# The first stage of a decoder block laid down in a fixed order for every engine

## The chip, the cores and the metric

The kernel runs on one core of a Trainium2 chip. The metric is device microseconds from start to end of one execution. Five engines work side by side, each through its own list of instructions in order: PE (TensorE, the matmuls), ACT (ScalarE), DVE (VectorE), POOL (GpSimd) and SP (SyncE, which here only issues loads and stores). An instruction that waits for another engine or for a transfer holds up all that stand behind it in its own list.

## What is computed

One decoder layer on 512 tokens of width 1024, in float32. The stage that is changed is the first: the norm of x, its transposes, and the projection to values and branch gates.

```python
h = rmsnorm(x, norm_mix[l])
proj = h @ w_in[l]
(qa, ka, va, qb, kc, vc, ksl, vsl, kw, vw, g_nsa, g_a, g_b) = jnp.split(proj, IN_OFFSETS, axis=-1)
y_a = swa_sink_attention(heads(qa, A_HEADS), heads(ka, A_KV_HEADS), heads(va, A_KV_HEADS),
                         attn_sinks[l], table_a)
...
nsa_gates = jax.nn.sigmoid(g_nsa).reshape(bsz, seq, B_KV_GROUPS, B_HEADS // B_KV_GROUPS, 3)
...
merged = jax.nn.sigmoid(g_a) * (y_a @ w_up_a[l]) + jax.nn.sigmoid(g_b) * (y_b @ w_up_b[l])
x = x + merged @ w_out[l]
h = rmsnorm(x, norm_ffn[l])
ug = causal_dwconv(h @ w_ffn_in[l], conv_w[l], conv_b[l])
...
x = x + (jax.nn.silu(g) * u) @ w_ffn_out[l]
```

The attentions add a bias from a table of 32 distance buckets by 16 heads (`rel_bias_table`).

## The kernel before

Each float32 operand of a matmul is split into a high part (a rounded copy, made on ACT, L79) and a low part (what is left, made on DVE or POOL, L80), and a product is three matmuls: high by high, high by low, low by high (L91 to L93).

The **first stage** takes the tokens in four blocks of 128. For each block `norm_x` (L152) squares both halves of x on ACT (`junk`), sums and scales them on DVE (`ssq`), takes the power -0.5 on POOL (`rstd_n`), multiplies x by it and by the norm's weights on DVE (L161), and has PE transpose the eight 128 by 128 pieces into two banks (`tp_x`, two groups of four), whose high and low parts (`xTh`, `xTl`) ACT and DVE take out. The norm's weights reach all partitions by a matmul of a column of ones with the loaded row (`gam`, L112, from `grow`). `values` (L171) then multiplies a block with the weights of the value and gate columns, 408 of them (`wvr` as loaded, in two halves of the model width; `wvh`, `wvl` split): 24 matmuls `v` for each block, 96 in all. The block's result is taken out by ACT and DVE in turn as `VA`, `VB` and the gates (`eg`); only then is its bank free.

Behind it come the **projections** of keys and queries (`p_ka`, `p_qa`, `p_kc`, ...), 24 matmuls for each 128 columns, with weights loaded through a ring of three (`raw_ka`, `raw_qa`, ...) and split (`hl_ka`, ...), and then, between the projections, the attention. `p_ka` takes the bank that the third token block's values have left.

The **distance table** is a matmul of the bucket table with a one-hot matrix (`pg`, L419, from `tab` and `og`, in pieces of 384, 512 and 128 columns) that ACT copies out (L420); SP writes it 32 times over to memory (`gdr`, L421, 1 MB from 8 partitions) and reads it back shifted (`TA`, L427).

All loads are issued by SP. In its queue each one waits until the load eight issues ahead of it has landed. What stands where in an engine's list is set by a scheduler that goes by priorities and a model of the times; in the first stage too. The low part of half of `wvr` and of `raw_ka` is split off on POOL (`POOLJ`, L26, L191).

Of the kernel before, what the change touches and what calls it, by code (L numbers as in the profile page):

```python
# [48 lines left out]

def hybrid(tc, x, wv, wblk, w1, w2, wua, wub, wout, wfi, wfo, nmix, nffn, nfin, sinks, par, table, onehot, out):  # L50
# [9 lines left out]
    with es:  # L60
# [16 lines left out]

        def split(hi, lo, src, eng=None):
# [24 lines left out]
        for h in range(2):  # L103
            sl = slice(h * 512, (h + 1) * 512)
            nc.sync.dma_start(xt[0][:, sl], x[0:P, sl])
            if h == 0:
                nc.sync.dma_start(grow, nmix)
        ones = C.tile([1, P], F32, name="ones")
        V.memset(ones, 1.0)
        gam = [bank("sc", f"gam{h}") for h in range(2)]  # L110
        for h in range(2):
            T.matmul(gam[h], ones, grow[:, h * 512 : (h + 1) * 512], start=True, stop=True)  # L112
# [3 lines left out]
        nc.sync.dma_start(wvr[0], wv[0])  # L116
        nc.sync.dma_start(xt[1], x[P : 2 * P])
        nc.sync.dma_start(wvr[1], wv[1])
        for t in range(2, NT):
            nc.sync.dma_start(xt[t], x[t * P : (t + 1) * P])  # L120
# [738 lines left out]
```

## Time and profile before

| | |
|---|---|
| three runs | 776.62, 777.75 and 781.49 us, median 777.75 |
| the profiled execution: span from first to last instruction | 779.1 us |
| instructions | 9688 |
| mean granted clock of TensorE over the span | 0.982 |

Of the profiled execution only the span is recorded, not a time of its own beside it. The span lies within the three runs, 1.4 us above their median, so the profile can stand for a usual run; a difference worked out against its span is carried over to the median.

### The profile page before, as it was taken

Reading aid. Unit: us, or ns where it says so; the run is one execution under the profiler, and the core shown is the slowest. Engines: PE = TensorE matmul, PEld = TensorE weight load, DVE = VectorE, ACT = ScalarE, POOL = GpSimd, SP = SyncE. Lnnn points to the kernel's source line nnn. Section 1 sums busy time; section 2 is a strip of 40 time slices with the busy share of each in tenths; the row PEclk is TensorE's granted clock in tenths of the full one; section 3 lists DMA queues with packets and bytes.
Section 4 is the critical chain, followed back from the end, with each engine's and each line's share of the span. In section 5 each row is a group of like instructions: output and inputs, shape, how many; then the busy total and the mean of one; then the engine's idle time right before and its main releaser. Section 6 shows DMA issues by size and latency. Waiting matters only on the chain.

```text
span 779.1 us, 9688 instructions
## 1 busy us (share of the span) xinstructions
PE 755.7 (97%) x3566; PEld 622.9 (80%) x3566; DVE 458.7 (59%) x921; ACT 370.9 (48%) x684; POOL 156.0 (20%) x125
## 2 busy tenths in 40 slices
PE   7999989899999999989999999999999999999996
PEld 5788778787887878768889888888888888888885
DVE  5527988746875567668755666565665555224123
ACT  7335685645666765546333534444443443213113
POOL 5024536324423344321500000000000000002001
PEclk9899998999999999999999999999999999999998
DMA  8463335421121211123502423323232233232302
GB/s 301 94 138 119 101 99 165 125 82 55 32 77 55 82 56 52 66 99 128 170 1 82 136 89 100 105 85 108 84 107 93 96 109 119 98 108 81 109 28 108
DMA packets 24182, 76.74 MB, mean 98 GB/s; under 512 B 3748, under 2 KB 4900, under 8 KB 24134
## 3 DMA queue, kind: packets, MB, share of 16 engines
q1 hardware_dynamic: 24134, 76.12, 30.6%
q8 instruction: 28, 0.46, 0.2%
q14 instruction: 20, 0.16, 0.1%
HBM read 72.96 MB, written 3.15 MB: 98 GB/s over the span
## 4 chain that ended last, share of the span: by engine, by line
PE 90%; DVE 6%; POOL 1%; issue 1%; ACT 1%; DMA 1%; SPq 0%; POOLq 0%; DVEq 0%; ACTq 0%
PE ug L92 10%; PE ug L93 10%; PE ug L91 10%; PE fo L753 5%; PE fo L752 5%; PE fo L754 5%; PE pT L454 3%; PE up L91 2%; PE p_gb L93 2%; PE up L93 2%; PE up L92 2%; PE p_gb L91 2%; PE p_gb L92 2%; PE wo L92 2%; PE wo L91 2%; PE wo L93 2%
## 5 line engine op out<-in xcount | busy, mean ns | idle before, releaser
L92 PE MATMUL ug<-hTl,hl_fi 128*128 128x512 f32 (+1 forms) x376 | 141.1, 375 | 0.0
L93 PE MATMUL ug<-hTh,hl_fi 128*128 128x512 f32 (+1 forms) x376 | 141.1, 375 | 0.0
L91 PE MATMUL ug<-hTh,hl_fi 128*128 128x512 f32 (+1 forms) x376 | 140.9, 376 | 0.0
L92 PEld LDWEIGHTS ug<-hTl,hl_fi 128*128 128x128 f32 x376 | 70.8, 188 | 12.9
L91 PEld LDWEIGHTS ug<-hTh,hl_fi 128*128 128x128 f32 x376 | 70.6, 188 | 12.9
L93 PEld LDWEIGHTS ug<-hTh,hl_fi 128*128 128x128 f32 x376 | 70.8, 188 | 12.6
L736 ACT ACTIVATE cv<-ug,prm 128x512 f32<-128x512 f32 x44 | 34.4, 782 | 96.0 <-PE ug L93 96.0
L737 DVE SCALAR_TENSOR_TENSOR cv<-ug,prm,cv 128x511 f32<-128x511 f32 x44 | 33.0, 750 | 77.0 <-ACT cv L736 76.9
L753 PE MATMUL fo<-hl_fo,AH 128*128 128x512 f32 x176 | 68.5, 389 | 0.0
L752 PE MATMUL fo<-hl_fo,AH 128*128 128x512 f32 x176 | 67.3, 389 | 0.0
L80 DVE TENSOR_TENSOR hl_fo<-raw_fo,hl_fo 128x1024 fp32r<-128x1024 f32 x22 | 27.1, 1235 | 64.6 <-ACT hl_fo L79 64.6
L778 POOL TENSOR_TENSOR X<-X,nfin 128x512 f32<-128x512 f32 x4 | 5.2, 1318 | 296.7 <-ACT junk L776 296.7
L80 DVE TENSOR_TENSOR ptl<-pT,pth 128x512 fp32r<-128x512 f32 (+4 forms) x62 | 41.8, 685 | 30.5 <-ACT pth L79 25.5
L80 DVE TENSOR_TENSOR hl_fi<-raw_fi,hl_fi 128x1024 fp32r<-128x1024 f32 x44 | 53.5, 1217 | 1.8 <-ACT hl_fi L79 1.8
L79 ACT CAST hl_fo<-raw_fo 128x1024 fp32r<-128x1024 f32 x22 | 23.2, 1054 | 65.6 <-PE fo L754 65.6
L376 ACT ACTIVATE Pb<-Pb,nmb 128x512 f32<-128x512 f32 (+3 forms) x64 | 35.9, 561 | 35.2 <-DVE nmb L447 34.9
L754 PE MATMUL fo<-hl_fo,AL 128*128 128x512 f32 x128 | 49.8, 389 | 0.0
L79 ACT CAST hl_fi<-raw_fi 128x1024 fp32r<-128x1024 f32 x44 | 45.7, 1041 | 2.4 <-PE wo L93 2.4
L79 ACT CAST pth<-pT 128x512 fp32r<-128x512 f32 (+4 forms) x62 | 35.2, 583 | 20.3 <-PE pT L454 15.6
L587 POOL TENSOR_TENSOR Pb<-Pb,smb 128x512 f32<-128x512 f32 (+3 forms) x32 | 25.9, 829 | 65.2 <-DVE smb L571 45.3
L752 PEld LDWEIGHTS fo<-hl_fo,AH 128*128 128x128 f32 x176 | 33.0, 188 | 6.9
L753 PEld LDWEIGHTS fo<-hl_fo,AH 128*128 128x128 f32 x176 | 33.0, 188 | 6.8
(308 smaller groups left out, 1727.3 us busy)
## 6 DMA issues: line engine op xcount, KB each, us to landing
raw_fi<-in_wfi_dram SPq DMA_DIRECT2D x44, 512.0 KB, 3.3
raw_fo<-in_wfo_dram SPq DMA_DIRECT2D x22, 512.0 KB, 3.2
raw_w<-in_w_dram SPq DMA_DIRECT2D x8, 512.0 KB, 3.6
raw_ga<-in_wblk_dram SPq DMA_DIRECT2D x8, 512.0 KB, 3.3
raw_gb<-in_wblk_dram SPq DMA_DIRECT2D x8, 512.0 KB, 3.2
raw_wo<-in_wout_dram SPq DMA_DIRECT2D x5, 512.0 KB, 3.7
raw_qa<-in_wblk_dram SPq DMA_DIRECT2D x4, 512.0 KB, 5.0
raw_qb<-in_wblk_dram SPq DMA_DIRECT2D x4, 512.0 KB, 6.1
```

The lines of the kernel that those rows point to most:

```text
L79: A.copy(hi, src)
L80: (eng or V).tensor_tensor(lo, src, f(hi), op=ALU.subtract)
L91: T.matmul(ps, wh, xh, start=start, stop=False)
L92: T.matmul(ps, wh, xl, start=False, stop=False)
L93: T.matmul(ps, wl, xh, start=False, stop=stop)
L376: last_exp[0] = A.activation(a[0], a[1], AF.Exp, **k)
L587: G.tensor_tensor(pr[r][:, :n], pr[r][:, :n], sm[:, r : r + 1].to_broadcast([P, n]), op=ALU.mult)
L736: A.activation(c, ps, AF.Identity, scale=cw(2, blk), bias=cb(blk))
L737: V.scalar_tensor_tensor(c[:, 1:], ps[:, : S - 1], cw(1, blk), c[:, 1:], op0=ALU.mult, op1=ALU.add)
L752: T.matmul(po[t], ah, wh, start=(k == 0), stop=False)
L753: T.matmul(po[t], ah, wl, start=False, stop=False)
L754: T.matmul(po[t], al, wh, start=False, stop=(k == NF - 1))
```

## The change

The first stage is written out instruction by instruction, under a switch that makes the scheduler keep that order on every engine. Against before:

- PE begins with twelve transposes of the identity (`early`) whose results nobody reads; then come `gam`, the whole table product `pg` (in banks of the tag `pt`, not `sc`), and then the first block of x.
- The row of the norm, the bucket table and the one-hot matrix are loaded from ACT's queue; the other loads stay on SP. The sinks (`nsink`) are loaded ahead of the first projection's weights, the table is written (`gdr`) right behind the small loads `cx`.
- The value weights are split in four pieces of 816 columns: high parts on ACT between the other steps, low parts on DVE; POOL splits nothing in this stage, and `ka` leaves `POOLJ`, so that its low part is made on DVE too.
- The high and low parts of projection weights may not stand ahead of the last block's transposed parts on their engines (`issue_after`).

```diff
         def split(hi, lo, src, eng=None):
-            A.copy(hi, src)
-            (eng or V).tensor_tensor(lo, src, f(hi), op=ALU.subtract)
+            xparts.append(A.copy(hi, src))
+            xparts.append((eng or V).tensor_tensor(lo, src, f(hi), op=ALU.subtract))
...
-        norm_x(0)
-        VA = slot(16, [P, NT, 2, P], F32R, "VA")
-        for h in range(2):
-            split(wvh[h], wvl[h], wvr[h], (G, None)[h])
-        for t in range(1, NT):
-            norm_x(t)
-            values(t - 1)
-        values(NT - 1)
...
+        def wv_hi(h, c):
+            A.copy(wvh[h][:, 2 * c : 2 * c + 2], wvr[h][:, 2 * c : 2 * c + 2])
+
+        def wv_lo(h, c):
+            cs = slice(2 * c, 2 * c + 2)
+            V.tensor_tensor(wvl[h][:, cs], wvr[h][:, cs], f(wvh[h])[:, cs], op=ALU.subtract)
...
+        with tc.manual_schedule():
...
+            nc.scalar.dma_start(grow[:, :D], nmix)
+            nc.scalar.dma_start(tab[:32], table)
+            nc.scalar.dma_start(oh, onehot)
...
+            for i in range(3):
+                pw = bank("pt", f"early{i}")
+                for c in range(4):
+                    T.transpose(pw[:, c * P : (c + 1) * P], ident, ident)
+            gam = [bank("sc", f"gam{h}") for h in range(2)]
...
+            pgs = []
+            for c0, c1, h0 in ((0, ZA, 0), (ZA, ZA + 512, 8), (ZA + 512, ZA + ZW, 8)):
+                pgs.append((bank("pt", f"pg{c0}"), c0, c1))
+                T.matmul(pgs[-1][0][:8, : c1 - c0], tab[:, h0 : h0 + 8], oh[:, c0:c1], start=True, stop=True)
+            squares(0)
+            scaled(0)
+            for pg, c0, c1 in pgs:
+                A.copy(gsb[:, c0:c1], pg[:8, : c1 - c0])
+            for c in range(2):
+                wv_hi(0, c)
+                transposed(xt[0], xTh, xTl, 0, c, "x")
+            values(0, 0, False)
+            squares(1)
+            wv_lo(0, 0)
+            wv_lo(0, 1)
+            values(0, 0, True)
+            wv_hi(1, 0)
+            wv_hi(1, 1)
+            scaled(1)
+            values(0, 1, False)
+            for t in range(1, NT):
+                transposed(xt[t], xTh, xTl, t, 0, "x")
+                if t == 1:
+                    wv_lo(1, 0)
+                    wv_lo(1, 1)
+                if t + 1 < NT:
+                    squares(t + 1)
+                values(t - 1, 1, True)
+                transposed(xt[t], xTh, xTl, t, 1, "x")
+                xlast = xparts[-2:]
+                if t + 1 < NT:
+                    scaled(t + 1)
+                values(t, 0, False)
+                values_out(t - 1)
+                values(t, 0, True)
+                values(t, 1, False)
+            values(NT - 1, 1, True)
+            values_out(NT - 1)
...
         def filler():
-            i, nxt = 0, jobs[0][1]()
+            with tc.issue_after(xlast[0].ins), tc.issue_after(xlast[1].ins):
+                i, nxt = 0, jobs[0][1]()
```

`squares`, `scaled` and `values_out` are the parts of `norm_x` and `values` under names of their own; `values(t, h, low)` is the part of block t's 24 matmuls that uses half h of the model width, without or with the weights' low part.

The beginning of PE's list, before (`_86` and the like are buffer numbers; `x_79` holds the first two blocks):

```order
L112 MATMUL gam_86<-grow,ones 128x512
L112 MATMUL gam_87<-grow,ones 128x512
L144 MATMUL tp_x_0_127<-ident,x_79 128x128 x4
L144 MATMUL tp_x_1_135<-ident,x_79 128x128 x4
L177 MATMUL v_173<-wvh_92,xTh_110 128x408 x4
L177 MATMUL v_173<-wvh_92,xTl_112 128x408 x4
L177 MATMUL v_173<-wvh_93,xTh_111 128x408 x4
L177 MATMUL v_173<-wvh_93,xTl_113 128x408 x4
```

Here the first block's transposes follow the norm's broadcast at once.

On PE after, a dozen transposes and the table product come first; `x_75` holds the first two blocks there:

```order
L212 MATMUL early_121<-ident 128x128 x4
L212 MATMUL early_126<-ident 128x128 x4
L212 MATMUL early_131<-ident 128x128 x4
L215 MATMUL gam_136<-grow 128x512
L215 MATMUL gam_137<-grow 128x512
L219 MATMUL pg_140<-og,tab 8x384
L219 MATMUL pg_142<-og,tab 8x512
L219 MATMUL pg_144<-og,tab 8x128
L131 MATMUL tp_x_0_162<-ident,x_75 128x128 x4
L131 MATMUL tp_x_1_170<-ident,x_75 128x128 x4
L174 MATMUL v_177<-wvh_83,xTh_91 128x408 x4
L174 MATMUL v_177<-wvh_83,xTl_93 128x408 x4
```

The table product, which stood between the second and third block's transposes, now stands ahead of the first, behind twelve transposes that are new.

The end of the stage in ACT's list, before (`v_292` is the third block's bank, `v_325` the fourth's):

```order
L79 CAST xTh_110<-tp_x_0_277 128x4x128
L79 CAST VB<-v_233 128x4x64
L79 CAST xTh_111<-tp_x_1_285 128x4x128
L182 ACTIVATE eg_262<-v_233 128x24
L79 CAST VA<-v_292 128x2x64
L79 CAST VB<-v_292 128x4x64
L182 ACTIVATE eg_321<-v_292 128x24
L79 CAST VA<-v_325 128x2x64
L79 CAST VB<-v_325 128x4x64
L182 ACTIVATE eg_354<-v_325 128x24
L319 CAST KA<-p_ka 64x512
```

Between the third block's `VA` and its gates stands only its `VB`.

The same place on ACT after (`v_306` is the third block's bank, `tp_x_1_346` the last transposes of x):

```order
L81 CAST xTh_91<-tp_x_0_335 128x4x128
L81 CAST xTh_92<-tp_x_1_346 128x4x128
L81 CAST VA<-v_306 128x2x64
L81 CAST hl_ka<-raw_ka 128x1024
L81 CAST hl_qa_404<-raw_qa_402 128x1024
L81 CAST hl_qa_455<-raw_qa_453 128x1024
L81 CAST VB<-v_306 128x4x64
L183 ACTIVATE eg_366<-v_306 128x24
L81 CAST VA<-v_353 128x2x64
L81 CAST VB<-v_353 128x4x64
L183 ACTIVATE eg_390<-v_353 128x24
L378 CAST KA<-p_ka 64x512
```

Three casts of projection weights, which stood earlier, between the first blocks, now stand between the third block's `VA` and its `VB` and gates; DVE's three low parts stand in the same place in its list.

SP's queue around the table's write, before:

```order
L412 DMA og<-in_onehot_dram 33x1024
L415 DMA cx<-in_w_dram 128x2x64 x4
L85 DMA raw_qa_432<-in_wblk_dram 128x1024
L85 DMA raw_kc<-in_wblk_dram 128x1024
L85 DMA raw_qa_509<-in_wblk_dram 128x1024
L421 DMA gdr<-og 8x32x1024
L85 DMA raw_w_0_0_610<-in_w_dram 128x1024
L427 DMA TA<-gdr 32x8x256 x4
```

Three weight loads stand ahead of the write, one between it and `TA`.

The same place in SP's queue after:

```order
L87 DMA raw_qa_402<-in_wblk_dram 128x1024
L466 DMA cx<-in_w_dram 128x2x64 x4
L468 DMA gdr<-og 8x32x1024
L87 DMA raw_qa_453<-in_wblk_dram 128x1024
L87 DMA raw_kc<-in_wblk_dram 128x1024
L474 DMA TA<-gdr 32x8x256 x4
L87 DMA raw_qa_530<-in_wblk_dram 128x1024
L87 DMA raw_w_0_0_631<-in_w_dram 128x1024
```

The write of the table has moved ahead of the weights of `qa1` (`raw_qa_432` before, `raw_qa_453` after) and of `kc`. Behind this, from `p_ka` on, the lists of PE, ACT, DVE and POOL are the same as before.

## Rows read from the trace of the kernel before

**Rows 1.** page, part 1: busy us (share of the span) and instructions per engine

```profile
PE 755.7 (97%) x3566; PEld 622.9 (80%) x3566; DVE 458.7 (59%) x921; ACT 370.9 (48%) x684; POOL 156.0 (20%) x125
```

**Rows 2.** windows, one stretch: busy us per engine, granted clock, DMA share, GB/s

```profile
40.28:100.00 59.72, 58.13 (x282) 47.74 (x282) 39.66 (x102) 33.54 (x75) 23.90 (x17) 0.97 0.44 118
```

**Rows 3.** chain of waits, 0 to 57 us: start us, us, what

```profile
9.08 3.69 POOL wvl L80
...
13.06 2.13 POOL rstd_n L137
...
30.61 0.44 PE tp_x L144 x4
...
32.23 8.21 PE v L177 x44
```

**Rows 4.** timeline of PE: start us, us, what, idle before and releaser

```profile
3.35 3.75 PE L112 MATMUL gam<-grow,ones 1*128 1x512 f32 x4 [3.35 <-DMA grow<-in_nmix_dram]
7.71 1.97 PE L144 MATMUL tp_x<-ident,x 128*128 128x128 f32 x8 [0.61 <-DVE x L161]
9.54 1.73 PE L177 MATMUL v<-wvh,xTh 128*128 128x408 f32 x4
...
14.83 1.65 PE L177 MATMUL v<-wvl,xTh 128*128 128x408 f32 x8
...
21.10 3.15 PE L419 MATMUL pg<-og,tab 33*8 33x384 f32 x4 [1.39 <-DVE x L161]
...
40.28 0.40 PE L91 MATMUL p_ka<-xTh,hl_ka 128*128 128x512 f32 x1
```

**Rows 5.** windows of 1 us, PE alone: busy us, granted clock, DMA share, GB/s

```profile
21.00:22.00 1.00, 0.90 (x2) 0.50 0.68 172
```

**Rows 6.** timeline of POOL

```profile
1.02 0.29 POOL masks.py:199 TENSOR_SCALAR_AFFINE_SELECT ident<-ident 128x128 f32<-128x128 f32 x1
```

**Rows 7.** timeline of ACT

```profile
7.45 1.55 ACT L79 CAST wvh<-wvr 128x1632 fp32r<-128x1632 f32 x1 [1.60 <-DMA wvr<-in_wv_dram]
...
10.01 0.58 ACT L79 CAST xTh<-tp_x 128x512 fp32r<-128x512 f32 x1
...
14.06 0.60 ACT L156 ACTIVATE junk<-x 128x512 f32<-128x512 f32 x1
...
16.68 1.05 ACT L79 CAST hl_ka<-raw_ka 128x1024 fp32r<-128x1024 f32 x1
...
28.20 0.26 ACT L420 COPY og<-pg 8x128 f32<-8x128 f32 x1 [2.28 <-PE pg L419]
...
37.48 0.19 ACT L182 ACTIVATE eg<-v 128x24 f32<-128x24 f32 x1 [0.49 <-DVE VB L80]
```

**Rows 8.** timeline of DVE

```profile
12.91 1.86 DVE L80 TENSOR_TENSOR wvl<-wvr,wvh 128x1632 fp32r<-128x1632 f32 x1
15.21 1.41 DVE L161 SCALAR_TENSOR_TENSOR x<-x,rstd_n,gam 128x512 f32<-128x512 f32 x2 [0.45 <-POOL rstd_n L137]
...
21.63 0.68 DVE L80 TENSOR_TENSOR xTl<-tp_x,xTh 128x512 fp32r<-128x512 f32 x1
...
23.16 1.21 DVE L80 TENSOR_TENSOR hl_qa<-raw_qa,hl_qa 128x1024 fp32r<-128x1024 f32 x1
...
37.03 0.42 DVE L80 TENSOR_TENSOR VB<-v,VB 128x256 fp32r<-128x256 f32 x1 [0.44 <-ACT VB L79]
```

**Rows 9.** tile view of tab, 0 to 75 us: time from issue to landing

```profile
DMA to landing us min/median/max: 8.0/8.0/8.0
```

**Rows 10.** timeline of SP, the queue of loads

```profile
16.33 0.35 SPq L85 DMA_DIRECT2D raw_qa<-in_wblk_dram  x1
...
28.48 0.31 SPq L421 DMA_DIRECT2D gdr<-og  x1
28.89 0.33 SPq L85 DMA_DIRECT2D raw_w<-in_w_dram  x1
```

**Rows 11.** tile view of raw_w, 28 to 52 us: time from issue to landing

```profile
DMA to landing us min/median/max: 22.7/22.7/22.7
```

More of the change, by code (lines that the diff above doesn't have):

```diff
@@ L102, in hybrid @@
         xt = [(x01, x23)[t // 2][:, t % 2] for t in range(NT)]
-        for h in range(2):
[L104 to L112, printed above, removed]
+        halves = [slice(0, 512), slice(512, 1024)]
+        grow = slot(6, [1, D + P], F32, "grow")
+        ones = grow[:, D:]
+        tab = C.tile([33, 16], F32, name="tab")
+        og = slot(15, [33, 2, ZA + ZW], F32, "og")
+        oh, gsb = og[:, 0], og[:8, 1]
+        nsink = C.tile([P, 8], F32, name="nsink")
         wvr = [slot(7 + h, [P, 4, NV], F32, f"wvr{h}") for h in range(2)]
@@ L115, in hybrid @@
         wvl = [slot(11 + h, [P, 4, NV], F32R, f"wvl{h}") for h in range(2)]
[L116 to L120, printed above, removed]
+        warm = C.tile([P, 1], F32, name="warm")
+        mhalf = C.tile([P, 1], F32, name="mhalf")
         ident = C.tile([P, P], F32, name="ident")
-        make_identity(nc, ident)
-        mhalf = C.tile([P, 1], F32, name="mhalf")
-        V.memset(mhalf, -0.5)
         prm = C.tile([P, par.shape[1]], F32, name="prm")
-        nc.sync.dma_start(prm, par)
         cw = lambda tap, blk: prm[:, tap * 44 + blk : tap * 44 + blk + 1]
@@ L149, in hybrid, with squares @@
         xTl = [slot(2 + h, [P, 4, S], F32R, f"xTl{h}") for h in range(2)]
-        halves = [slice(0, 512), slice(512, 1024)]
-        def norm_x(t):
+        xh = lambda k: xTh[k // 4][:, k % 4]
+        xl = lambda k: xTl[k // 4][:, k % 4]
+        VB = slot(13, [P, NT, 4, P], F32R, "VB")
+        gate = C.tile([P, NT, 3, 8], F32, name="gate")
+        VA = slot(16, [P, NT, 2, P], F32R, "VA")
+        st_x, st_v = {}, {}
+        def squares(t):
             s2 = SM.tile([P, 2], F32, tag="s2", name=f"s2x_{t}")
@@ L158, in norm_x, with scaled, values, values_out @@
             V.tensor_tensor(ssq, s2[:, 0:1], s2[:, 1:2], op=ALU.add)
-            r = rstd_of(ssq, f"n1_{t}")
+            st_x[t] = rstd_of(ssq, f"n1_{t}")
+        def scaled(t):
             for h in range(2):
-                V.scalar_tensor_tensor(xt[t][:, halves[h]], xt[t][:, halves[h]], r, gam[h], op0=ALU.mult, op1=ALU.mult)
-                transposed(xt[t], xTh, xTl, t, h, "x")
-        xh = lambda k: xTh[k // 4][:, k % 4]
-        xl = lambda k: xTl[k // 4][:, k % 4]
-        VB = slot(13, [P, NT, 4, P], F32R, "VB")
-        gate = C.tile([P, NT, 3, 8], F32, name="gate")
-        def values(t):
-            ps = bank("mm", f"v{t}")
-            sl = slice(t * P, (t + 1) * P)
-            order = [(i, k) for h in range(2) for i in (0, 2) for k in range(4 * h, 4 * h + 4)] + [(1, k) for k in range(KD)]
-            for n, (i, k) in enumerate(order):
-                h, kk = k // 4, k % 4
-                T.matmul(ps[:, :NV], (xh, xh, xl)[i](k)[:, sl], (wvh, wvl, wvh)[i][h][:, kk], start=(n == 0), stop=(n == 23))
+                V.scalar_tensor_tensor(xt[t][:, halves[h]], xt[t][:, halves[h]], st_x[t], gam[h], op0=ALU.mult, op1=ALU.mult)
+        def wv_hi(h, c):
[3 more added lines that the diff above has]
+            V.tensor_tensor(wvl[h][:, cs], wvr[h][:, cs], f(wvh[h])[:, cs], op=ALU.subtract)
+        def values(t, h, low):
+            if t not in st_v:
+                st_v[t] = bank("mm", f"v{t}")
+            sl = slice(t * P, (t + 1) * P)
+            for i in ((1,) if low else (0, 2)):
+                for k in range(4 * h, 4 * h + 4):
+                    T.matmul(st_v[t][:, :NV], (xh, xh, xl)[i](k)[:, sl], (wvh, wvl, wvh)[i][h][:, k % 4],
+                             start=(h == 0 and i == 0 and k == 0), stop=(h == 1 and i == 1 and k == 7))
+        def values_out(t):
+            ps = st_v[t]
             pv = ps[:, 0:384].rearrange("p (n d) -> p n d", d=64)
@@ L416, in hybrid @@
         gdr = DR.tile([COPIES, 8, ZA + ZW], F32, name="gdr")
-        for c0, c1, h0 in ((0, ZA, 0), (ZA, ZA + 512, 8), (ZA + 512, ZA + ZW, 8)):
-            pg = bank("sc", f"pg{c0}")
-            T.matmul(pg[:8, : c1 - c0], tab[:, h0 : h0 + 8], oh[:, c0:c1], start=True, stop=True)
-            A.copy(gsb[:, c0:c1], pg[:8, : c1 - c0])
         nc.sync.dma_start(gdr.rearrange("c h z -> h c z"), gsb[:, None, :].to_broadcast([8, COPIES, ZA + ZW]))
```

35 lines of the change are left out of this document (20 added, 15 removed).

## The prediction

> **What bounds the kernel now.** I began with the page's busy shares: PE is busy for 755.7 of 779.1 us [rows 1], so a change can move the end only where PE stands still, runs at the lower clock, or does work that needn't be done. The second view was the window from the first projection on: between 40.28 and 100 us PE is busy for 58.13 of 59.72 us [rows 2]. As the lists of PE, ACT, DVE and POOL are the same in both kernels from `p_ka` on, whatever the first stage gains or loses is carried to the end, and the quantity to predict is the moment at which `p_ka` starts: 40.28 us now [rows 4].
>
> The third view, the chain of waits over the first stage, says what sets that moment. In its first half PE is not on it: the chain runs through POOL's low part of the value weights (3.69 us) and a `rstd_n` on POOL that takes 2.13 us [rows 3] while DVE makes the other low part [rows 8]. From 21.1 us on it is PE to the end: the table product, then value matmuls and transposes [rows 3, 4]. So the stage is not purely bound by PE: 96 value matmuls at 8.21/44 = 0.187 us [rows 3] are 17.9 us, and eight groups of transposes at 0.44 us are 3.5 us [rows 3], out of 40.28.
>
> The fourth view is PE's timeline with the granted clock. The first value matmuls took 1.73 us for four, 0.43 each; from 14.83 us on eight took 1.65, 0.2 each [rows 4]: the first stretch ran at 1.2 GHz, whatever the record says of it, the second at 2.4. The table product then stood waiting for 1.39 us for a bank that DVE's last scaling of x frees, and ran at a granted clock of 0.50, that is 1.2 GHz [rows 4, 5].
>
> **The change part by part.** What it takes from the chain: POOL's 3.69 us, the 2.13 us of `rstd_n`, the wait of 1.39 us and the product's 3.15 us in mid-stage: 10.4 us gross. What it puts in their place has to be followed from the start.
>
> 1. PE's front. The identity is ready at 1.02 + 0.29 = 1.3 us [rows 6]. Twelve transposes at 1.97/8 = 0.25 us, the price in the cold first stretch [rows 4], are 3.0 us: 4.3 us. Then `gam`, 3.75 us [rows 4]: 8.0, where before it ended at 7.1. Then the table product: 896 columns took 3.15 us at 1.2 GHz [rows 4], so 1024 take 3.6: 11.6 us. That the one-hot matrix has landed by 8.0 is an assumption. Its load isn't seen in this position; `tab`, 2 KB, took 8.0 us behind the big loads on SP [rows 9], while the norm's row was there at 3.35 us [rows 4]. Issued near 2 us it lands between 4 and 10, and costs between 0 and 2.0 us. I take 0, by the norm's row: it is nearest, a load at the head of a short queue.
>
> 2. ACT behind it. ACT's list holds the three copies of the product ahead of everything else of the first block, so ACT stands from its squares of block 0 until PE is through: the last copy (0.26) [rows 7] ends at 11.9 us. Then the two casts of the first half of the weights (together 1.55) and two of `xTh` (0.58 each): 14.6 us; before, the second of these ended at 10.6 [rows 7]. Then the squares of block 1, 2 x 0.60 [rows 7]: 15.8 us.
>
> 3. DVE behind that. Both low pieces of the first half stand behind `ssq` of block 1: 1.86 us for 1632 columns in one piece [rows 8], the same in two: 17.7 us. Then the scaling of block 1, 1.41 [rows 8]: 19.1 us. POOL's 3.69 us are gone, and so is its overlap with DVE; but this 1.86 us now stands in the way of block 1.
>
> 4. PE to the end of block 0. Two matmuls on the last piece: 18.1 to 18.5. Eight of the second half: 1.5 us at 2.4 GHz, 3.1 to 3.5 at 1.2: 19.6 to 21.6. One group of block 1's transposes, 0.44 to 1.0: 20.0 to 22.6. Then PE waits for ACT's `xTh` (0.58), DVE's `xTl` (0.68) and both low pieces of the second half (1.86) [rows 7, 8]: 23.1 to 25.7, and its last two matmuls end at 23.5 to 26.5 us. Before, block 0 was done at 14.83 + 1.65 = 16.5 [rows 4].
>
> 5. PE's remainder. From there it has 72 matmuls (13.5) and five groups of transposes (2.2): 15.7 us if it neither waits nor slows: 39.2 to 42.2. In the old kernel the same work, with the table product and one more group of transposes, took 40.28 - 16.48 = 23.8 us.
>
> 6. The last bank. `p_ka` needs the third block's bank, which the gates free last, and between that block's `VA` and `VB` now stand three casts of weights on ACT and three low parts on DVE. They come behind the last transposes of x, which end 24 x 0.187 = 4.5 us before PE's values do: at 34.7 to 37.7. From there: `xTh` 0.58, the first cast 1.05, three low parts of 1.21, `VB`'s 0.42, the gates' 0.19 [rows 7, 8]: 5.9 us, so `p_ka` starts at 40.6 to 43.6 us, 1.4 us after PE has run dry. In the old kernel nothing stood there. I take 42.5, a little above the middle, because steps of 0.1 to 0.3 us are left out.
>
> The rest costs nothing: the loads on ACT's queue delay its first square by some tenths, which the second half of x covers; `ka`'s low part on DVE is counted in 6; `gdr` and `TA` come earlier, but the first scores stand behind `qa1` in PE's list either way.
>
> The sum: 42.5 - 40.28 = +2.2 us on a span of 779.1, and on the median 777.75 + 2.2 = **780.0 us**: the 10.4 us are given back. Three runs spread by 4.9 us; a difference under 1% is about what a measurement of this kernel can't tell from no change.
>
> **The clock and the warm-up transposes.** In the old trace PE was hardly idle from 3.35 us on (0.61 us between `gam` and the first transposes), and yet the value matmuls at 9.54 us still ran at 1.2 GHz [rows 4]; the product at 21.1 us also ran at the lower clock [rows 5]. So neither had raised it. The Trainium skill (TensorE: Matmul & The Clock Gate, Part 4: PE-mode transpose) says that transposes don't count as busy for the clock in the same way, which speaks against the twelve: by it they only delay `gam` by 0.9 us and the sum stands; no row here shows transposes alone. If twelve more do raise the clock, the first rival below follows.
>
> **Rivals.**
>
> Early clock (faster). If PE runs at 2.4 GHz from about 4 us, the product ends at 4.3 + 1.9 + 1.8 = 8.0 us instead of 11.6, every later step comes 3.6 us sooner and takes the lower ends: 40.6 - 3.6 = 37.0, a gain of 3.3 us: 774.5 us. For it: PE's front is now without a gap. Against: `gam` ran for 3.75 us and raised nothing.
>
> A load behind the table's write (slower). `gdr` is slow: in the old kernel the weight load issued 0.4 us behind it took 22.7 us to land [rows 10, 11]. Now `qa1`'s weights stand in that place, and their cast stands on ACT ahead of the third block's `VB` and gates. If `gdr` is issued at g, `qa1` lands at g + 23.1 and `p_ka` can't start before g + 23.1 + 1.05 + 1.21 + 0.42 + 0.19 = g + 26.0. It decides from g = 16.5 us; beyond, each microsecond costs one. The old queue was past the same four `cx` loads at 16.33 us [rows 10], and three loads ahead of them are gone, so I expect g near 15 and `qa1` at 38, just in cover. If SP or ACT's copies are later, say g = 20, the time is 783.5; at the old place, g = 28.5, it is 792.
>
> No trace at all. PE's 1.6 us of idling before 100 us [rows 2] could absorb part of a shift: 778.
>
> **How the numbers follow.** The forecast, 778.5 to 782, has 0.58; the early clock, 773.5 to 777, 0.24; the load behind the write, 782 to 792, 0.12; no trace, 0.06. Faster by over 1% (under 770) needs the early clock and more than its price: 0.03. Slower by over 1% (over 785.5) needs g beyond 22: 0.04. Within 1%: 0.93. The range runs from 773.5, the early clock less a microsecond of spread, to 785, the load rival at g = 21.5; that takes in the 2.0 us of a late one-hot matrix.
>
> **What the profile will show.** If I am right, PE's timeline has `gam` ending near 8.0 and `pg` near 11.6 at the price of 1.2 GHz, ACT idle on `pg` until near 11 us, PE waiting for `wvl` between 16 and 25 us, and at the end on the third block's gates behind three casts. Step 1 is wrong if `pg` takes 1.8 us, or starts late on its load; step 6 is wrong if `p_ka` follows the last value matmul at once, or if the cast of `qa1` waits for its load. The forecast as a whole is wrong if `p_ka` starts before 39 or after 45 us, or if the time behind `p_ka` differs by more than 2 us between the kernels.

## The result and the profile after

| | before | after |
|---|---|---|
| median, first measurement (8 runs each) | 778.2 us | 784.91 us |
| ratio of the times, 95% interval | | 1.0077 [1.0054, 1.01] |
| median, second measurement (35 and 12 runs) | 779.45 us | 784.62 us |
| ratio, second measurement | | 1.0064 [1.004, 1.0087] |
| profiled execution: span | 779.1 us | 783.9 us, a second one 781.0 us |
| start of `p_ka` | 40.28 us | 45.26 us, in the second profile 42.12 us |

The change makes the kernel 0.6 to 0.8% slower, 5 to 7 us. The forecast was 780.0 us, in a range of 773.5 to 785.0: right in its direction and in that the difference stays within 1%, and too small by 3 to 5 us. The measured 784.91 us lies 0.1 us inside the upper end of the range. A few executions took 1.09 to 2.5 times as long as the rest (847.81 to 1930.3 us) and are left out of the ratios and of the comparisons of single runs.

PE's line on the page (busy us, share of the span, instructions), and the window of the same length as [rows 2], from `p_ka` on (PE, PEld, DVE, ACT, POOL, granted clock, DMA share, GB/s):

```profile
PE 759.0 (97%) x3578; PEld 625.7 (80%) x3578; DVE 457.5 (58%) x925; ACT 370.2 (47%) x686; POOL 149.2 (19%) x123
```

```profile
45.26:104.98 59.72, 58.13 (x280) 47.78 (x281) 39.88 (x102) 33.23 (x74) 23.87 (x17) 0.97 0.40 123
```

PE is busy for 58.13 of 59.72 us there, to the hundredth what it was [rows 2]. From `p_ka` to the end it is 783.9 - 45.26 = 738.6 us, and was 779.1 - 40.28 = 738.8. So in these two executions the whole difference arises ahead of `p_ka`.

PE's timeline after, to be held against [rows 4] (start us, us, what, idle before and releaser):

```profile
4.11 3.78 PE L215 MATMUL gam<-grow 1*128 1x512 f32 x4
8.67 3.57 PE L219 MATMUL pg<-og,tab 33*8 33x384 f32 x6 [0.78 <-DMA og<-in_onehot_dram]
12.17 1.97 PE L131 MATMUL tp_x<-ident,x 128*128 128x128 f32 x8
13.96 1.81 PE L174 MATMUL v<-wvh,xTh 128*128 128x408 f32 x4
...
17.90 0.64 PE L174 MATMUL v<-wvl,xTh 128*128 128x408 f32 x2 [1.38 <-DVE wvl L165]
...
25.25 0.64 PE L174 MATMUL v<-wvl,xTh 128*128 128x408 f32 x2 [2.31 <-DVE wvl L165]
26.17 1.05 PE L174 MATMUL v<-wvl,xTh 128*128 128x408 f32 x2 [0.28 <-DVE wvl L165]
...
43.01 0.91 PE L174 MATMUL v<-wvl,xTh 128*128 128x408 f32 x4
45.26 0.50 PE L93 MATMUL p_ka<-xTh,hl_ka 128*128 128x512 f32 x1 [1.34 <-ACT eg L183]
```

The first value matmul starts at 13.96 instead of 9.54 us, PE waits four times for low pieces from DVE (4.3 us with the two of 0.28), and at the end 1.34 us for the third block's gates. ACT, DVE and SP show where these waits come from:

```profile
11.85 0.73 ACT L223 COPY og<-pg 8x512 f32<-8x512 f32 x2 [1.24 <-PE pg L219]
...
45.02 0.19 ACT L183 ACTIVATE eg<-v 128x24 f32<-128x24 f32 x1 [1.73 <-DVE VB L82]
```

```profile
16.84 1.92 DVE L165 TENSOR_TENSOR wvl<-wvr,wvh 128x816 fp32r<-128x816 f32 x2
18.68 1.40 DVE L158 SCALAR_TENSOR_TENSOR x<-x,rstd_n,gam 128x512 f32<-128x512 f32 x2
...
24.20 1.92 DVE L165 TENSOR_TENSOR wvl<-wvr,wvh 128x816 fp32r<-128x816 f32 x2
...
42.30 2.35 DVE L82 TENSOR_TENSOR hl_qa<-raw_qa,hl_qa 128x1024 fp32r<-128x1024 f32 x2
```

```profile
15.63 0.72 SPq L468 DMA_DIRECT2D gdr<-og  x1
16.52 0.36 SPq L87 DMA_DIRECT2D raw_qa<-in_wblk_dram  x1
```

The second profile of the same kernel has the same waits (1.17, 2.32 and 1.35 us), but not the same clock:

```profile
8.50 3.57 PE L219 MATMUL pg<-og,tab 33*8 33x384 f32 x6 [0.61 <-DMA og<-in_onehot_dram]
...
17.73 0.63 PE L174 MATMUL v<-wvl,xTh 128*128 128x408 f32 x2 [1.17 <-DVE wvl L165]
...
23.54 0.63 PE L174 MATMUL v<-wvl,xTh 128*128 128x408 f32 x2 [2.32 <-DVE wvl L165]
...
42.12 0.50 PE L93 MATMUL p_ka<-xTh,hl_ka 128*128 128x512 f32 x1 [1.35 <-ACT eg L183]
```

Windows of 2 us, PE alone (busy us, granted clock, DMA share, GB/s), of the first profile and then of the second:

```profile
20.00:22.00 2.00, 2.00 (x8) 0.50 0.49 59
...
26.00:28.00 2.00, 1.83 (x7) 0.50 0.52 55
```

```profile
20.00:22.00 2.00, 1.22 (x9) 1.00 0.48 55
...
26.00:28.00 2.00, 2.00 (x13) 1.00 0.48 51
```

In the first, 6.8 us of the stage after the head run at a granted clock of 0.50, that is 1.2 GHz; in the second none. That is nearly all of the 3.1 us between 45.26 and 42.12; 0.2 us is the one-hot matrix, which came that much sooner.

### The profile page after: what moved, and what is told of

Same layout as the page of the kernel before. It is cut to its first block, busy times and chain, and to the rows that moved or that the text cites. A ratio compares the mean times of both kernels' runs of the same rounds, so it can differ in the third digit from the quotient of the medians.

```text
span 783.9 us, 9720 instructions
## 1 busy us (share of the span) xinstructions
PE 759.0 (97%) x3578; PEld 625.7 (80%) x3578; DVE 457.5 (58%) x925; ACT 370.2 (47%) x686; POOL 149.2 (19%) x123
## 3 DMA queue, kind: packets, MB, share of 16 engines
HBM read 72.96 MB, written 3.15 MB: 97 GB/s over the span
## 4 chain that ended last, share of the span: by engine, by line
PE 90%; DVE 6%; DMA 2%; ACT 1%; issue 1%; SPq 0%; POOL 0%; POOLq 0%; DVEq 0%; ACTq 0%
PE ug L93 10%; PE ug L95 10%; PE ug L94 10%; PE fo L801 5%; PE fo L799 5%; PE fo L800 5%; PE pT L501 3%; PE up L93 2%; PE up L94 2%; PE p_gb L95 2%; PE up L95 2%; PE p_gb L93 2%; PE p_gb L94 2%; PE wo L95 2%; PE wo L94 2%; PE wo L93 2%
## 5 line engine op out<-in xcount | busy, mean ns | idle before, releaser
L81 ACT CAST pth<-pT 128x512 fp32r<-128x512 f32 (+4 forms) x62 | 35.1, 583 | 20.2 <-PE pT L501 15.7
L634 POOL TENSOR_TENSOR Pb<-Pb,smb 128x512 f32<-128x512 f32 (+3 forms) x32 | 25.9, 828 | 65.1 <-DVE smb L618 45.3
```

The source lines that it names most:

```text
L81: xparts.append(A.copy(hi, src))
L634: G.tensor_tensor(pr[r][:, :n], pr[r][:, :n], sm[:, r : r + 1].to_broadcast([P, n]), op=ALU.mult)
```

## The experiments

All profiled executions in one table. "At 1.2 GHz" is worked out from windows of 1 us: twice what the granted clock lacks of 1, summed over the stage ahead of `p_ka` and over what is behind it. Over the head of the stage the record says 1.00, though the prices there are those of 1.2 GHz (`gam` at 3.75 us), so the head is not in the column; and 1.5 to 4.7 us of what is behind stand at the end of the span, after PE's last matmul, where they cost nothing. "Behind" is the span less the start of `p_ka`. The ratio is to the kernel before, in runs taken together with it.

| kernel | `p_ka` us | at 1.2 GHz: stage, behind | behind us | median us | ratio [95%] |
|---|---|---|---|---|---|
| before | 40.28 | 6.8, 21.1 | 738.8 | 778.2 to 779.45 | |
| after | 45.26 | 6.8, 20.7 | 738.6 | 784.91 | 1.0077 [1.0054, 1.01] |
| c0_after_again | 42.12 | 0.0, 21.0 | 738.9 | 784.62 | 1.0064 [1.004, 1.0087] |
| e1_no_early | 42.65 | 3.4, 4.9 | 734.0 | 785.25 | 1.0063 [1.0036, 1.009] |
| e2_low_early | 41.90 | 0.0, 14.8 | 736.5 | 779.95 | 1.002 [0.9999, 1.0042] |
| e3_product_late | 42.22 | 3.4, 20.7 | 738.6 | 781.52 | 1.0015 [0.9987, 1.0043] |
| e4_casts_free | 55.69 | 13.6, 11.6 | 734.5 | 791.41 | 1.015 [1.0121, 1.018] |
| e5_write_on_act | 40.92 | 0.0, 5.4 | 734.1 | 778.23 | 1.0002 [0.9975, 1.0029] |
| e7_all_mended | 37.12 | 0.0, 20.9 | 739.8 | 774.95 | 0.9961 [0.9935, 0.9988] |
| e8_early_matmuls | 45.17 | 13.6, 20.9 | 738.5 | 784.76 | 1.0071 [1.004, 1.0102] |
| e9_mended_warm | none | none | none | 779.78 | 0.9999 [0.9974, 1.0024] |
| e10_casts_staged | 44.32 | 6.8, 4.9 | 733.9 | 779.8 | 1.0005 [0.9982, 1.0028] |
| b1_low_on_dve | 38.35 | 3.4, 5.2 | 734.1 | 777.21 | 0.9978 [0.9951, 1.0005] |
| b2_shifted | 45.37 | 6.8, 19.1 | 740.3 | 786.03 | 1.0079 [1.0047, 1.0111] |

Two things are read from it. A time is the start of `p_ka` plus what lies behind it, and what lies behind it goes with the clock: 733.9 to 734.5 us where 5 to 12 us run at 1.2 GHz, 736.5 at 15, 738.5 to 740.3 at 19 to 21. So one profile tells what a change does to the stage by `p_ka`, once the clock in the stage is the same; its total can be 5 us off by the clock behind `p_ka`.

The medians mix the two in the same way, and the mean clock recorded with each run takes them apart. Held against runs of the kernel before with the same mean clock (to 0.001), the spans are on average longer by 3.9 us for the changed kernel (9 of its 20 runs have such a partner), 4.1 for e1, 3.6 for e2, 3.1 for e10, 3.9 for e8, 1.4 for e3 (-0.8 to 2.7) and 5.9 for b2. For b1 they are the same (-0.1), and for e7 shorter by 0.9 (between 3.2 shorter and 1.7 longer). So at the same clock e2 gives back 0.3 us of the changed kernel's loss, e10 0.8 and e7 4.8, about what their `p_ka` says; the rest of the differences between the medians goes with the clock that the runs had.

**e1_no_early: the twelve transposes.**

```diff
-            for i in range(3):
-                pw = bank("pt", f"early{i}")
-                for c in range(4):
-                    T.transpose(pw[:, c * P : (c + 1) * P], ident, ident)
```

> The changed kernel without the twelve early transposes; all else in place. Theory (they only fill time in which PE would wait): gam starts at 3.4 us instead of 4.1, but the product still stands until the one-hot matrix lands near 8.6, so p_ka starts where it did, 45.3 +- 0.4, and the time is that of the changed kernel, 784.9 +- 1. Rival (they bring the higher clock sooner): without them the stretch of 2.4 GHz that begins at 15.9 us comes later and p_ka starts 1 to 3 us later, at 46.3 to 48. Second rival (they hold the loads or the front back): p_ka earlier by 0.7 us or more.

Median 785.25 us: as the theory has it, the time of the changed kernel. `p_ka` at 42.65 us in the one profile isn't. That execution was the shortest of its runs by 5.7 us (778.45); half of the stage's stretches at 1.2 GHz are missing in it, and the one-hot matrix came 1.2 us sooner:

```profile
2.47 3.75 PE L211 MATMUL gam<-grow 1*128 1x512 f32 x4 [2.47 <-DMA grow<-in_nmix_dram]
7.49 3.57 PE L215 MATMUL pg<-og,tab 33*8 33x384 f32 x6 [1.27 <-DMA og<-in_onehot_dram]
```

`gam` and the product take what they took behind the transposes (3.75 and 3.57 us here, 3.78 and 3.57 there), and PE waits for the matrix either way. The first rival falls: without the transposes the mean clocks are no lower (0.982 to 0.995, against 0.976 to 0.988). The second, 0.7 us or more, holds for this one profile and not for the median.

**e2_low_early: the low pieces earlier.**

```diff
-            squares(1)
             wv_lo(0, 0)
             wv_lo(0, 1)
-            values(0, 0, True)
             wv_hi(1, 0)
             wv_hi(1, 1)
+            wv_lo(1, 0)
+            squares(1)
+            wv_lo(1, 1)
+            values(0, 0, True)
             scaled(1)
...
-                if t == 1:
-                    wv_lo(1, 0)
-                    wv_lo(1, 1)
```

> The changed kernel with the low pieces of the value weights earlier in DVE's list: both of the first half and the first of the second half ahead of the sum of squares of block 1, the last ahead of block 1's scaling, and ACT's two casts of the second half ahead of the squares of block 1. Theory (PE's waits of 1.4, 0.3, 2.3 and 0.3 us for these pieces are the price of DVE's order): they go, block 1 comes about 1 us later on DVE without being late for PE, and p_ka starts 2.5 to 4 us sooner, at 41.3 to 42.8; time 781 to 782.4. Rival (the clock is what costs): PE still runs the rest of block 0 and block 1 at 1.2 GHz, and p_ka gains under 1.5 us. Second rival (the wait moves to block 1's scaled x): PE waits 1.5 us or more for x or its transposed parts and p_ka gains under 1.5 us.

Median 779.95 us, 5 us less than the changed kernel, and less than the theory's 781. PE's last value matmul ends at 38.4 us instead of 43.9 (40.8 in the second profile, at the same clock), and then a new wait opens on PE and ACT:

```profile
37.47 0.91 PE L174 MATMUL v<-wvl,xTh 128*128 128x408 f32 x4
41.90 0.50 PE L93 MATMUL p_ka<-xTh,hl_ka 128*128 128x512 f32 x1 [3.52 <-ACT eg L183]
```

```profile
38.99 1.04 ACT L81 CAST hl_qa<-raw_qa 128x1024 fp32r<-128x1024 f32 x1 [2.51 <-DMA raw_qa<-in_wblk_dram]
```

The theory of DVE's order holds for the four waits (only 0.28 us is left, and 1.16 us for block 1's x). What was expected of `p_ka` came, but by another sum: 2.4 us gained ahead of the last bank at the same clock, and 2.2 of them lost to the second rival of the prediction, the load of `qa1` behind the table's write. So `p_ka` is only 0.2 us sooner than in the second profile, and most of the 5 us on the median is the clock: 0.988 to 0.995 in these runs, 0.976 to 0.988 in those of the changed kernel.

**e3_product_late: the product behind the first block.**

```diff
-            pgs = []
-            for c0, c1, h0 in (...):
-                (bank and T.matmul of pg)
...
-            for pg, c0, c1 in pgs:
-                A.copy(gsb[:, c0:c1], pg[:8, : c1 - c0])
...
+                if t == 1:
+                    (the same loops, pg and its copies)
                 values(t - 1, 1, True)
```

> The changed kernel with the table product and its three copies moved back behind the first block (PE: ahead of the two low matmuls on the last pieces; ACT: behind the squares of block 2); SP then has qa1's load ahead of the table's write. Theory (the product at the head of the lists holds ACT's casts, and with them everything of block 0, back by 3.5 to 4.4 us): the first value matmul starts near 9.5 to 10.5 instead of 13.96, the product costs 1.9 to 3.6 us again in mid-stage, of which the wait for the low pieces hides up to 2.3; p_ka starts at 41.5 to 43.8. Rival (the end of the stage is set by the loads or by the three late casts, whatever the front does): p_ka starts within 1 us of 45.3.

```profile
10.91 1.82 PE L174 MATMUL v<-wvh,xTh 128*128 128x408 f32 x4 [1.06 <-ACT xTh L81]
...
19.88 1.88 PE L241 MATMUL pg<-og,tab 33*8 33x384 f32 x6
22.27 0.63 PE L174 MATMUL v<-wvl,xTh 128*128 128x408 f32 x2 [0.50 <-DVE wvl L165]
...
42.22 0.50 PE L93 MATMUL p_ka<-xTh,hl_ka 128*128 128x512 f32 x1 [1.34 <-ACT eg L183]
```

As the theory expects: the first value matmul comes 3.05 us sooner, the product costs 1.88 us at 2.4 GHz and fills most of the wait for the low pieces (0.50 us is left of 2.31). Median 781.52 us, 3.4 less than the changed kernel's first. `p_ka` at 42.22 us lies in the theory's range, but not at the clock of the second profile (3.4 us at 1.2 GHz in the stage, none there), so the two starts don't tell the gain; at the same mean clock it is about 2.5 us. The load of `qa1`, ahead of the write here, landed in 5.3 us, not 22.8. Its tile view in the changed kernel, then in this one:

```profile
DMA to landing us min/median/max: 22.8/22.8/22.8
```

```profile
DMA to landing us min/median/max: 5.3/5.3/5.3
```

**e4_casts_free: the casts not held back.**

```diff
-            with tc.issue_after(xlast[0].ins), tc.issue_after(xlast[1].ins):
-                i, nxt = 0, jobs[0][1]()
+            i, nxt = 0, jobs[0][1]()
...
-                    with hp(i >= HPJ), tc.issue_after(xlast[0].ins), tc.issue_after(xlast[1].ins):
+                    with hp(i >= HPJ):
```

> The changed kernel without the rule that issues the casts of ka, qa0 and qa1 behind the last parts of x: ka's and qa0's casts then stand on ACT in the first blocks, qa1's ahead of the transposed block 1's second half; qa1's load still stands behind the table's write on SP. Theory of the forecast with its second rival (a load behind that write takes 22.8 us): ACT stands on qa1's load until about 39 us, with block 1's transposed x behind it, and p_ka starts 15 to 25 us later, at 60 to 70; time 800 to 810. Rival (the write costs the loads behind it nothing as such, they were only not needed sooner): the three casts at the end cost 1.3 us and their going gives back 1 to 2, p_ka at 43.3 to 44.5.

```profile
39.25 1.04 ACT L81 CAST hl_qa<-raw_qa 128x1024 fp32r<-128x1024 f32 x1 [15.87 <-DMA raw_qa<-in_wblk_dram]
```

```profile
40.83 1.73 PE L174 MATMUL v<-wvh,xTh 128*128 128x408 f32 x4 [11.30 <-ACT xTh L81]
```

The mechanism is the theory's: ACT stands for 15.87 us on `qa1`'s load, PE behind it for 11.30. `p_ka` starts at 55.69 us, 10.4 later and not 15 to 25: by then PE had done block 0 and the first half of block 1, and at the end it waited for nothing. The median is 791.41 us, not 800 or more. So holding the casts back is right as long as the write stands ahead of that load.

**e5_write_on_act: the write on another queue.** e2_low_early with one line changed:

```diff
-        nc.sync.dma_start(gdr.rearrange(...), ...)
+        nc.scalar.dma_start(gdr.rearrange(...), ...)
```

> The kernel with the early low pieces (the second experiment), and the write of the table issued on ACT's queue instead of SP's. There p_ka waited 3.5 us because qa1's load landed 22.8 us after it was issued on SP behind that write. Theory (the load stands behind the write in one queue): on another queue the write no longer holds it, qa1 lands by 30 us, PE waits 1.0 to 1.6 us for the gates behind the three late casts, and p_ka starts at 39.2 to 40.4 instead of 41.9. Rival (the write crowds the DMA engines, whatever queue it is issued on): qa1 still lands after 35 us and p_ka starts at 41 to 43.

The tile view of `raw_qa` for this load (issue to landing), and the windows of 6 us behind it (granted clock, DMA share, GB/s):

```profile
DMA to landing us min/median/max: 21.9/21.9/21.9
```

```profile
24.00:30.00 6.00, 1.00 0.48 52
```

The theory of the queue falls. On a queue of its own the load of `qa1` still takes 21.9 us, issued at 15.81 and landed at 37.7. From 24 to 30 us the DMA engines are on average 0.48 busy and move 52 GB/s; in the changed kernel it is the same picture, 0.48 and 54 GB/s between 20 and 26 us. So the load is held up while the write (1 MB from eight partitions) runs, whichever of the two queues it is issued on; by what, these traces don't show. `p_ka` at 40.92 us lies between the two expectations: the write was issued 1.5 us sooner, and PE waits 1.28 us for the gates, but ACT's list now waits ahead of the issue, and the first value matmul comes at 15.07, after 1.77 us for `xTh`.

**e7_all_mended: all the places at once.** e1, e2 and e3 together, the loads of `tab` and of the one-hot matrix back at the end of SP's list, and the casts staged:

```diff
-            nc.scalar.dma_start(tab[:32], table)
-            nc.scalar.dma_start(oh, onehot)
...
+            nc.sync.dma_start(tab[:32], table)
+            nc.sync.dma_start(oh, onehot)
             nc.sync.dma_start(prm, par)
...
-            with tc.issue_after(xlast[0].ins), tc.issue_after(xlast[1].ins):
+            with tc.issue_after(xst[1][0].ins), tc.issue_after(xst[1][1].ins):
...
+                    aft = xst[2] if i == 1 else xlast + [gts[2]]
```

> The changed kernel mended at every place that cost something: no early transposes, product behind the first block, low pieces early, table and one-hot matrix loaded at the end of SP's list (the norm's row stays on ACT's queue), and the casts of ka, qa0 and qa1 placed behind block 1's x, block 2's x, and the last x and third block's gates. Theory (the first stage is a list of waits, each of which can be had back): first value matmul at 9 to 9.7, no wait above 1.2 us on the low pieces or on the gates, p_ka at 35.5 to 38.5; with 736 to 740 us behind it, time 773 to 777. Rival (the clock sets the stage, and PE's 1.2 GHz stretch only moves): p_ka at 39.5 to 41 and the time that of the kernel before within 1.5 us.

```profile
9.94 1.82 PE L175 MATMUL v<-wvh,xTh 128*128 128x408 f32 x4 [0.59 <-ACT xTh L81]
...
17.36 0.66 PE L131 MATMUL tp_x<-ident,x 128*128 128x128 f32 x4 [0.76 <-DVE x L159]
...
37.12 0.39 PE L93 MATMUL p_ka<-xTh,hl_ka 128*128 128x512 f32 x1
```

Median 774.95 us, `p_ka` at 37.12: the theory's numbers (the first value matmul, at 9.94, is a little later than its 9 to 9.7), and faster than both kernels, by 0.4% than the one before (0.9961 [0.9935, 0.9988]). No wait on low pieces or gates is left. Beside the kernel before most of the 4 us is the clock: the mean clocks are 0.987 to 0.995 here and go down to 0.982 there, and at the same mean clock the gain is about 1 us.

**e8_early_matmuls: real matmuls at the head.**

```diff
-                for c in range(4):
-                    T.transpose(pw[:, c * P : (c + 1) * P], ident, ident)
+                T.matmul(pw, wrm[:, :P], wrm, start=True, stop=True)
```

> The changed kernel with six matmuls of 128x512 on a constant tile in place of the twelve early transposes, all else in place (their result isn't used). Theory (nothing of 3 to 4 us at the head raises the clock in time): gam still takes 3.7 us and the product 3.5; PE waits less for the one-hot matrix; p_ka within 0.8 us of 45.3. Rival (the early clock: real matmuls would do what the transposes don't): gam or the product at half the price, 1.9 or 1.8 us, the first value matmul 1.5 to 3.5 us sooner than 13.96, and p_ka at 41.5 to 44.

```profile
1.51 2.93 PE L213 MATMUL early<-wrm 128*128 128x512 f32 x6 [1.51 <-DVE wrm L194]
4.37 2.30 PE L216 MATMUL gam<-grow 1*128 1x512 f32 x4
8.37 3.50 PE L220 MATMUL pg<-og,tab 33*8 33x384 f32 x6 [1.69 <-DMA og<-in_onehot_dram]
```

Median 784.76 us, that of the changed kernel. Each side is half right. Behind 2.93 us of matmuls `gam` takes 2.30 us, behind 2.82 us of transposes 3.78: by its price it ran at 2.4 GHz for a part behind the matmuls, and not behind the transposes. But PE then waits 1.69 us for the one-hot matrix, the product runs at 1.2 GHz again (granted clock 0.62 in the window from 8 to 10 us, then 0.50 to 14), and `p_ka` stays where it was, 45.17 us.

**e9_mended_warm: PE kept busy at the head of the mended kernel.**

```diff
+            busy(6)
             gam = [bank("sc", f"gam{h}") for h in range(2)]
...
+            busy(4)
             squares(0)
...
                 transposed(xt[0], xTh, xTl, 0, c, "x")
+                busy((2, 8)[c])
```

> The mended kernel (the one that starts p_ka at 37.1 us) with twenty matmuls of 128x512 on a constant tile, whose result isn't used, put where PE would stand or work at 1.2 GHz: six ahead of gam, four behind it, two and eight behind block 0's two groups of transposes. Theory (six such matmuls at the head had brought gam from 3.75 to 2.3 us, and the clock fell again only because PE then waited for the one-hot matrix): kept busy, PE runs block 0's first sixteen value matmuls at 0.19 to 0.25 us instead of 0.39 each, and p_ka starts 1.5 to 3.5 us sooner than 37.1, at 33.6 to 35.6; time 771.5 to 773.5. Rival (the loads and DVE set block 0, so a faster PE only waits): p_ka within 1 us of 37.1 and the time of the mended kernel, 775 +- 1.

Median 779.78 us, that of the kernel before, and 4.8 us above the mended kernel (774.95, on another chip, where the kernel before took 779.16 against 779.45 here). So the theory's gain isn't there, and the rival, which expected the mended kernel's time, isn't right either. That the extra matmuls cost something is likely but not shown cleanly: the intervals of the two ratios, [0.9974, 1.0024] and [0.9935, 0.9988], overlap, and at the same mean clock the difference is below 2 us. The one profiled execution took 1,930 us and says nothing of where it arises.

**e10_casts_staged: the casts alone.** The changed kernel with only the staging of e7_all_mended.

> The changed kernel with the three casts alone moved: ka's behind block 1's x, qa0's behind block 2's, qa1's behind the last x and the third block's gates (the load of qa1 stays behind the table's write). Theory (the three casts with their low parts in front of the third block's gates cost the 1.3 us by which p_ka waits at the end, and nothing more): PE's last wait goes, p_ka starts at 43.6 to 44.4. Rival (a cast in mid-stage holds block 2's or block 3's transposed x): PE waits there instead, and p_ka starts at 45 or later.

```profile
39.74 1.01 PE L175 MATMUL v<-wvh,xTh 128*128 128x408 f32 x4 [0.39 <-ACT xTh L81]
...
44.32 0.40 PE L93 MATMUL p_ka<-xTh,hl_ka 128*128 128x512 f32 x1
```

PE's last wait is gone and `p_ka` starts at 44.32, 0.9 us sooner at the same clock (0.4 of the 1.3 us comes back as a wait for `xTh`): the theory. The median, though, falls by 4.8 us beside the changed kernel on the same chip, 779.8 against 784.62. Behind `p_ka` it ran 4.9 us at 1.2 GHz, the changed kernel 21. Windows at the same distance from `p_ka`, of this kernel and then of the changed one:

```profile
95.00:99.00 4.00, 3.04 (x14) 1.00 0.26 74
```

```profile
96.00:100.00 4.00, 3.04 (x9) 0.69 0.27 71
```

PE is busy for the same 3.04 us of 4, behind the same wait of 0.96 us; the one execution keeps 2.4 GHz and gets through 14 matmuls, the other falls to 1.2 and gets through 9.

**b1_low_on_dve: one part alone on the kernel before.**

```diff
-        split(wvh[h], wvl[h], wvr[h], (G, None)[h])
+        split(wvh[h], wvl[h], wvr[h], None)
```

> The kernel before with one part of the change alone: DVE makes both low halves of the value weights, in whole pieces, and POOL none. Theory (POOL's 3.69 us lay beside PE's work at the low clock; block 0 was only done 16.5 us in, and PE sets the end from 21 us on): block 1's scaling comes up to 1.5 us later, p_ka within 1 us of 40.3, time within 1.5 us of the kernel before. Rival (POOL's share was what held the first blocks): p_ka 1.5 to 4 us sooner, at 36.3 to 38.8.

```profile
14.61 1.65 PE L177 MATMUL v<-wvl,xTh 128*128 128x408 f32 x8
...
20.70 1.68 PE L419 MATMUL pg<-og,tab 33*8 33x384 f32 x4 [1.20 <-DVE x L161]
...
38.35 0.40 PE L91 MATMUL p_ka<-xTh,hl_ka 128*128 128x512 f32 x1
```

Block 0 is done at 16.3 us instead of 16.5, so POOL's 3.69 us were no bound. `p_ka` came 1.9 us sooner, which lies in the rival's range and not in the theory's. But 1.5 of the 1.9 are the product, which ran at 2.4 GHz in this execution (1.68 us, 3.15 in [rows 4]), and at the same mean clock the spans are those of the kernel before. Median 777.21 us, not told apart from before.

**b2_shifted: the kernel before, 4.5 us later.**

```diff
         values(NT - 1)
+        late = bank("pt", "late")
+        for i in range(24):
+            T.matmul(late[:, :NV], xh(i % KD)[:, 384:], wvh[i % 8 // 4][:, i % 4], start=(i == 0), stop=(i == 23))
```

> The kernel before with 24 extra value matmuls of the last block into a bank of their own at the end of the first stage; their result isn't used. They are busy time of 24 x 0.187 = 4.5 us, so p_ka starts 4.5 us later and nothing else is changed. The changed kernel's profiled run starts p_ka 5.0 us later than the old one's, but its median is 6.7 us longer. Theory (the 1.7 us over and above come with a later p_ka, whatever made it late, as more stretches at 1.2 GHz behind it): median 5.5 to 7.5 us over the kernel before, and mean clocks mostly at 0.985 or less. Rival (they belong to the changed order of the first stage or of SP's loads, or to the draw of the runs): 4.0 to 5.0 us over, and mean clocks spread over 0.982 to 0.995 as in the kernel before.

`p_ka` at 45.37 us (+5.1), median 786.03 against 779.45. The time is the theory's (+6.6), the clocks are rather the rival's: runs from 0.983 to 0.992, five of eleven at 0.989 or more. The interval of the ratio, 1.0047 to 1.0111, is 3.7 to 8.7 us. Undecided.

**c0_after_again: the changed kernel once more.**

> The changed kernel once more, unaltered, beside the others. If the 6.7 us hold: 783.5 to 786 at a mean clock of 0.976 to 0.987, p_ka at 45.3, the product at 8.7. Rival (the first eight runs were a draw of the lower clock): some runs at 0.990 or more and a median of 781 to 783.

Median 784.62 us, mean clocks 0.976 to 0.988: the first measurement holds. Its `p_ka` at 42.12 instead of 45.3 was not expected, and is the second profile shown above.

## Why the prediction was right, point by point, and where it was short

**That the stage's work only changes places: right.** The 10.4 us gross were given back, and more. Each piece was found where the prediction had put it: the product at the head (3.57 us), ACT held behind its copies, DVE's pieces behind the sum of squares, PE waiting for `wvl`, the three casts in front of the gates. e2, e3 and e10 take these pieces out one at a time, and each gives its wait back (what e2 gained ahead of the last bank, the load of `qa1` took again); e7 takes out all and gains 5.0 us of `p_ka` on the second profile.

**Steps 1 to 3, mis-sized by 0.6 to 1.1 us.** `gam` ended at 7.9 (predicted 8.0) and the product took 3.57 (3.6), but it started at 8.67: the load of the one-hot matrix, for which the prediction took 0 out of 0 to 2.0, cost 0.78 us of waiting in the first profile, 0.61 in the second; by the prediction's own sign ("starts late on its load") step 1 was wrong there. The last copy ended at 12.6 (11.9), the second `xTh` at 15.2 (14.6), the low pieces at 18.8 (17.7): another 0.4 us is the sum of squares and `rstd` ahead of them on DVE, which the sum had left out.

**Steps 4 and 5, short by the clock in one execution of two.** Block 0 was predicted to end at 23.5 to 26.5, the remainder to take 15.7 us. In the second profile block 0 is done at 24.9 and PE's values end 15.8 us later; in the first it is 27.0 and 16.9, because 6.8 us ran at 1.2 GHz, the last of them behind block 0, where the forecast had 2.4 GHz ("if it neither waits nor slows"). The prediction had read the old product's 1.2 GHz as a clock that nothing had raised yet. Its own rows say otherwise: the value matmuls at 14.83 us ran at 2.4 GHz [rows 4], so the clock had come up and gone down again in mid-stage, and a fall of that kind had no term in step 5.

**Step 6, right.** From the end of the last transposes to `p_ka` it took 45.26 - 39.40 = 5.9 us (predicted 5.9), and PE stood 1.34 us (predicted 1.4).

**The start of `p_ka`.** Predicted 42.5; 42.12 in the second profile, 45.26 in the first, past the 45 us beyond which the forecast had called itself wrong. The median, too, lies where the prediction had put the load behind the write (782 to 792) and not in the forecast's own 778.5 to 782: the waits were the forecast's, their size and the clock weren't, and that the range still held 784.91, by 0.1 us, is partly luck. What lies behind it differs by no more than 0.3 us between the three profiles (738.6 to 738.9), as it had said, so the rival without a trace falls.

**From `p_ka` to the median: the term that was too small.** The prediction put its 2.2 us on the median, and took the profiled execution for a usual one, because its span lay 1.4 us above the median of the times. But a run's time is 1.7 to 1.9 us more than its span in every run that has both, so 779.1 us of span stand for some 780.9 us, 2.7 above the median of 778.2; at a mean clock of 0.982 it was one of the longer ones. Compared at the same mean clock, the changed kernel is 4.0 us longer: 783.9 against 780.0 us of span at 0.982 (4 and 24 runs), 782.3 against 778.3 at 0.984 (4 and 18). The rest of the 5 to 7 us is the clock: 45 of 91 runs of the kernel before had a mean of 0.989 or more, and none of 20 of the changed one. Why the changed order draws the lower clock more often isn't settled. A later `p_ka` alone didn't clearly do it (b2); with the casts staged the runs had 0.986 to 0.995 (e10), with the low pieces earlier 0.988 to 0.995 (e2); and the same place in the lists ran at either clock.

**The rivals.** The early clock didn't come: `gam` took 3.78 us behind 2.82 us of transposes, and 2.30 behind 2.93 us of matmuls (e8). The Trainium skill (TensorE: Matmul & The Clock Gate, Part 4: PE-mode transpose) says that transposes don't count as busy for the clock in the same way; this pair agrees with it. The load behind the write was there, in cover as forecast: `gdr` issued at 15.63 (g near 15), `qa1` landed 22.8 us after 16.52, at 39.3 (38), and ACT cast it later without waiting. e2 uncovered it, e4 made it the bound. The prediction priced it by its place behind the write; e5 shows that on another queue the load lands as late.

## What to carry to other kernels

A fixed order makes each engine's list wait for its slowest neighbour: what is put first on PE (here the product) also puts its copies first on ACT and everything behind them late, so follow every list to its next wait before moving anything up. A wait taken away shows the next one, and it may be a DMA that was in cover until then. Where a change is worth less than 1%, compare one landmark of the trace (here the start of `p_ka`) at the same granted clock, or single runs at the same mean clock, since runs differ by 5 us through the clock alone.

## What the runs showed that was not expected

The same program has stretches at 1.2 GHz in one execution and not in the next: the changed kernel's stage took 45.26 or 42.12 us. Behind `p_ka`, 5 us ran at 1.2 GHz in some kernels' profiles and 21 in others, at a cost of some 4.7 us (734.0 against 738.7). The stretches stand at fixed places: some 52, 76, 107 and 298 us behind `p_ka` in before, after, c0, e3, e7, e8 and b2, and at the second of these alone in e1, e5, e10 and b1. So most of these executions are of two kinds (e2 and e4 lie between); what decides between them isn't shown.

While 1 MB was written from eight partitions, the DMA engines moved 52 to 54 GB/s at a share of 0.48 (at that rate 1 MB takes some 20 us, an estimate), and a load of 512 KB issued beside it took 21.9 us on another queue, 22.8 on the same, and 5.3 when it was ahead of the write.
